# Block 1's transposes, the first W2 load and the order of VectorE's sums in the opening of a fused matmul-GELU-matmul kernel

## The chip, the cores and the metric

The kernel runs on one core of a Trainium2 chip. The metric is device time in microseconds (us) of one execution, the median of several. Each execution also reports its span, from first to last instruction, and the mean clock that was granted to TensorE, where 1.0 is full speed. The span is about 1.8 us shorter than the time. "PE" is TensorE, "PEld" its weight loads, "DVE" VectorE, "ACT" ScalarE, "POOL" GpSimd and "SP" the queue that issues most DMAs. bX, bY, bZ and bW are the banks of PSUM into which TensorE writes its products, and "arena" is the kernel's storage in SBUF.

## The reference

```python
def setup_inputs():
    batch, m, k, h, n = 16, 512, 768, 3072, 768
    # x (16, 512, 768), w1 (768, 3072), b1 (3072), w2 (3072, 768), all float32, random normal

def reference(x, w1, b1, w2):
    y = np.matmul(x, w1) + b1
    y = 0.5 * y * (1.0 + erf(y / np.sqrt(2.0)))
    return np.matmul(y, w2).astype(np.float32)
```

The 8192 rows of x are worked in eight blocks of 1024 rows. The change touches only the opening, in which blocks 0 and 1 are multiplied by W1.

## The kernel before

A block product is done with seven half-size products instead of eight (a Strassen-type scheme). This saves TensorE work and costs sums on VectorE. For x, they are S1, S2, a difference written over A21, and S4. For each W1 column tile there are four combinations, T1 to T4. A `Unit1` is one column tile of W1 times one block of x, and one call of `period` works on unit `i` and finishes unit `j`, the one before:

```python
            # period(i, j, fill), usual case
            p1(i); copy_xy(i)     # bX = A11*B11; ScalarE copies bX to bY
            p7(j)                 # bY of j += A21*T3; VectorE adds c22 (line 535)
            fill(1)
            p5(i)                 # bW = S1*T1; ScalarE copies bW out
            fill(2)
            p3(j)                 # bZ += S4*B22; VectorE adds c12 (line 562)
            fill(3)
            p6(i)                 # bY += S2*T2; VectorE copies bY to bZ (line 577), "the bZ copy"
            j.right_done(); fill(4)
            p4(j)                 # bY of j += A22*T4; GELU out of PSUM
            fill(5)
            p2(i); fill(6)        # bX += A12*B21; GELU out of PSUM
```

`p7` of the next period writes the bY bank that the bZ copy reads, so TensorE may not start it until that copy is done (TensorE waited 2.07 us for it in the longest case before). `fill(1)` to `fill(6)` put pending VectorE sums and DMA issues between the products. In the traces below VectorE works in the order in which the program gives it work, so a sum that waits for data holds back the bZ copy behind it (2.55 us in the largest case before the change).

```python
        def fill_a(pos, slot):                       # pos: place in the list of 24 Unit1 of blocks 0 and 1
            if slot == 1:
                if pos in (at[1, 0] - 2, at[1, 0] - 1):       # positions 5 and 6
                    h = pos - at[1, 0] + 2
                    x_sums(1, soon, slice(h * RH // 2, (h + 1) * RH // 2))   # sums of block 1
                if pos + 1 < len(seq) and seq[pos + 1][0] == 0:
                    prep_wt(seq[pos + 1][1])                  # T1..T4 of the next W1 tile
                ...
                for m, c in ((21, 9), (22, 0), (23, 3), (23, 6)):
                    if pos == m:
                        prep_w2(T2, c, queue)                 # combinations of W2
                ...
            elif slot in (1, 2, 4, 5):
                sums((0, 600, 300, 0, 600, 300)[slot])        # pop sums worth so many ns
            if slot == 5:
                loads_a(pos)
                if 1 <= pos < 5:
                    for t in (pos - 1, pos + 3):
                        transpose_dma(1, t)                   # one 128-row tile of block 1's x
            if slot == 6:
                flush(soon)
```

At this stage x, W1 and W2 come from HBM as float32 and are cast to float16 by DMAs that GpSimd issues. The row tiles of block 1 are then transposed from SBUF to SBUF by DMAs of SP, in the order 0, 4, 1, 5, 2, 6, 3, 7. The first half of block 1's sums needs the first four of them.

Of the kernel before, what the change touches and what calls it, by code (L numbers as in the profile page):

```python
# [10 lines left out]
P = 128  # L11
# [6 lines left out]
B11, B21, T1, B22, T3, T2, T4 = range(7)  # L18
# [4 lines left out]
def kernel(  # L23
# [8 lines left out]
    nc = tc.nc  # L32
# [5 lines left out]
    RH = SB // 2  # L38
    nsb = R // SB
    KQ = K // P // 2  # L40
    NH = H // P // 2
# [57 lines left out]
    def g_of(sb):  # L99
        return Gs[min(sb, 1)]  # L100
# [20 lines left out]
    def w1_op(wt, slot):  # L121
        raw = wt[:, 0:4 * KQ * P].rearrange("p (a k b c) -> p a b k c", a=2, k=KQ, b=2)
        if slot in RAW:
            return raw[:, RAW[slot][0], RAW[slot][1]]
        return wt[:, slot * KQ * P:(slot + 1) * KQ * P].rearrange("p (k c) -> p k c", c=P)
# [46 lines left out]
    bT = [pp.tile([P, 2 * KQ, P], F16, name=f"bT{k}") for k in range(2)]  # L172

    with tc.manual_schedule():

        soon, queue, late, slow = [], [], [], []

        def tt(o, a, b, op):
            nc.vector.tensor_tensor(out=o, in0=a, in1=b, op=op)  # L179

        def later(n, f, q=None):
            (queue if q is None else q).append((70 + n * 0.52, f))

        def sums(ns):

            for q in (soon, queue):
                while q and ns >= q[0][0] * 0.6:
                    ns -= q[0][0]
                    q.pop(0)[1]()

        def flush(q):
            while q:
                q.pop(0)[1]()
# [17 lines left out]
        def keep(n):  # L211
            nc.sync.dma_start(out=w1s[hi_of(n)][:], in_=wts[n])

        def prep_wt(n):
            o = {s: w1_op(wts[n], s) for s in range(7)}
            for d, a, b in ((T3, B22, T1), (T1, T1, B11), (T2, B22, T1), (T4, B21, T2)):
                later(KQ * P, lambda d=d, a=a, b=b: tt(o[d], o[a], o[b], SUB), soon)

        def load_w2(k, c0, c1):
            nc.gpsimd.dma_start(out=w2rows[k][:, c0:c1, :], in_=w2r[:, k, c0:c1, :])  # L220

        W2C = 3

        def prep_w2(d, c, q):
            a, b = {T1: (T3, B11), T2: (B22, T1), T3: (B22, T3), T4: (B21, T2)}[d]
            o = [w2v[s][:, :, c:c + W2C, :] for s in (d, a, b)]
            later(2 * W2C * N4, lambda: tt(*o, SUB), q)
# [49 lines left out]
        def xh_of(sb, t):  # L277
            if sb < ONE:
                return cut(sb * GR + GR // 2 + t * K, K)
            return xh_late[t % 3]  # L280
# [5 lines left out]
        def xT_of(sb, t):  # L286
            return XTs[sb][:, t // NU, :, (t % NU) * P:(t % NU + 1) * P]

        def transpose_dma(sb, t):
            nc.sync.dma_start_transpose(out=xT_of(sb, t), in_=xhs[t])  # L290

        def transpose_pe(t):
            for kc in range(2 * KQ):
                nc.tensor.transpose(out=bT[t % 2][:, kc, :], in_=xhs[t][:, kc * P:(kc + 1) * P],
                                    identity=ident[:])
            nc.scalar.copy(out=xT_of(0, t), in_=bT[t % 2][:])

        def blocks(sb):
            XT = XTs[sb]
            return [XT[:, a, c:c + KQ, :] for a in range(2) for c in (0, KQ)]  # L300

        def x_sums(sb, q, r=slice(0, RH)):
            A11, A12, A21, A22 = [a[:, :, r] for a in blocks(sb)]
            S1, S2, S4 = [a[:, :, r] for a in XSs[sb]]
            n = KQ * len(range(RH)[r])
            later(n, lambda: tt(S1, A21, A22, ADD), q)
            later(n, lambda: tt(S2, S1, A11, SUB), q)
            later(n, lambda: tt(A21, A11, A21, SUB), q)
            later(n, lambda: tt(S4, A12, S2, SUB), q)

        def g_sum(k, U, c0=0, c1=NH, q=None):
            G1, G2 = g_of(U // NU)
            r = slice(U % NU * P, (U % NU + 1) * P)
            g11, g21 = G1[:, c0:c1, 0, r], G1[:, c0:c1, 1, r]
            g12, g22 = G2[:, c0:c1, 0, r], G2[:, c0:c1, 1, r]
            s = [t[:, c0:c1, :] for t in GS]
            a, b, op = ((g21, g22, ADD), (s[0], g11, SUB), (g11, g21, SUB), (g12, s[1], SUB))[k]
            later((c1 - c0) * P, lambda: tt(s[k], a, b, op), q)
# [260 lines left out]
        def p2(u):  # L579
            u.mm(2, bX[u.g % 2], False, 0, u.C)  # L580
            u.alloc()
            u.left_done(0, bX[u.g % 2])
# [69 lines left out]
        def spin(n):  # L652

            for k in range(n):
                nc.tensor.matmul(out=warm[k % len(warm)][:], lhsT=zero[:, 0, 0:P], rhs=zero[:, 0, :],
                                 start=True, stop=True, skip_group_check=True)

        spin(9)
        for t in range(4):
            xhs[t] = xh_of(0, t)  # L660
            nc.vector.tensor_copy(out=xhs[t], in_=xf[:, t, :])
            transpose_pe(t)
            if t == 0:
                nc.tensor.transpose(out=bW[:, 0:2 * NH], in_=bf, identity=idf[0:2 * NH, 0:2 * NH])
                nc.scalar.copy(out=b1t[:], in_=bW[:, 0:2 * NH])
            spin(2 if t < 3 else 6)
# [8 lines left out]
        for t in range(4, 8):  # L675
            if t == 6:
                p2(first)
            transpose_pe(t)
            spin(2 if t < 7 else 6)
            x_sums(0, soon, slice((t - 4) * P, (t - 3) * P))  # L680
            flush(soon)


        seq = ([(0, k) for k in range(7)] +
               [(1, 0), (1, 1), (1, 2), (0, 7), (1, 3), (0, 8), (1, 4), (0, 9), (1, 6), (0, 10), (0, 11),
                (1, 5), (1, 10), (1, 11), (1, 7), (1, 8), (1, 9)])
        at = {u: n for n, u in enumerate(seq)}
        over = {7: 0, 8: 1, 9: 2, 10: 3, 11: 4}

        def load_next_x(sb, ts):  # L690
            for t in ts:
                load_x(sb, t)

        w2_at_pos = {7: (0, 0, 2), 9: (0, 2, 4), 11: (0, 4, 6), 13: (0, 6, 8),
                     at[1, 6] + 1: (0, 8, 10), at[1, 6] + 2: (0, 10, 12),
                     at[1, 5] + 1: (1, 7, 12), at[1, 10] + 1: (1, 0, 3), at[1, 11] + 1: (1, 3, 7)}

        def loads_a(pos):
            if pos == 0:
                load_wt(4)  # L700
                load_next_x(1, (0, 4, 1, 5))
                load_wt(5)
                load_next_x(1, (2, 6, 3, 7))
                load_wt(6)
            for n in range(7, NH):
                if pos == at[1, over[n]] + 1:
                    load_wt(n)
            if pos in w2_at_pos:
                load_w2(*w2_at_pos[pos])

        def fill_a(pos, slot):
            if slot == 1:
                if pos in (at[1, 0] - 2, at[1, 0] - 1):
                    h = pos - at[1, 0] + 2
                    x_sums(1, soon, slice(h * RH // 2, (h + 1) * RH // 2))
                if pos + 1 < len(seq) and seq[pos + 1][0] == 0:
                    prep_wt(seq[pos + 1][1])
                if pos == at[0, NH - 1] + 2:
                    for c in range(0, NH, W2C):
                        prep_w2(T1, c, queue)  # L720
                    for k in (0, 1):
                        g_sum(k, 0)
                for m, c in ((21, 9), (22, 0), (23, 3), (23, 6)):
                    if pos == m:
                        prep_w2(T2, c, queue)
                        prep_w2(T3, c, late if m == 23 else queue)
                if pos == 23:
                    for c in range(0, NH, W2C):
                        prep_w2(T4, c, late)
            if pos > at[0, NH - 1]:  # L730
                if slot in (1, 4):
                    sums((0, 1100, 0, 0, 1500)[slot])
            elif slot in (1, 2, 4, 5):
                sums((0, 600, 300, 0, 600, 300)[slot])
            if slot == 5:
                loads_a(pos)
                if 1 <= pos < 5:
                    for t in (pos - 1, pos + 3):
                        transpose_dma(1, t)
                if seq[pos][0] == 1:  # L740
                    keep(seq[pos][1])
            if slot == 6:
                flush(soon)
# [135 lines left out]
        for g, (kind, sb, k) in enumerate(units):  # L879
            cur = kind(g, sb, k) if g else first  # L880
            if g < len(seq):
                period(cur, prev, lambda slot: fill_a(g, slot))
            else:
                f = {Unit1: fill_mm1, Unit2: fill_mm2_one, Unit3: fill_mm2_two}[kind]
                period(cur, prev, lambda slot: f(sb, k, slot))
            prev = cur
# [30 lines left out]
```

## Time and profile before

The three runs at hand for the prediction had a median of 869.94 us (868.99 to 870.58). The profiled execution was 871.2 us with a span of 869.4.

These are lines of the profile page of before: the span, the engines' busy time, and the engines' shares of the chain that ended last ("issue" is time in which an engine waited for nothing that the profile shows; a "q" marks an engine's sequencer).

```profile
span 869.4 us, 16186 instructions
PE 853.5 (98%) x6298; PEld 560.2 (64%) x6298; DVE 653.0 (75%) x1114; ACT 418.9 (48%) x680; POOL 80.4 (9%) x131
...
PE 74%; DVE 14%; issue 6%; DMA 3%; ACT 1%; SPq 1%; POOL 0%; DVEq 0%; POOLq 0%
```

TensorE is the bottleneck, so only its gaps can be won. These lines are from the view of TensorE's waits: engine and line, what ended the wait, total us, number of times, and the longest.

```profile
PE bY L370 <- DVE bZ L577: 4.5, 4, 2.1
PE bY L462 <- DVE bZ L572: 2.1, 6, 0.3
PE bW L370 <- DVE arena L179: 1.5, 2, 0.8
```

The first line is the bZ copy, holding back `p7` four times. The longest of these waits is this one, in the timeline of TensorE (start, length, what, count, and in brackets the idle time before it):

```profile
40.50 1.46 PE L370 MATMUL bX<-arena 128*128 128x512 f16 x6
44.03 0.81 PE L370 MATMUL bY<-arena 128*128 128x512 f16 x3 [2.07 <-DVE bZ L577]
45.62 1.46 PE L370 MATMUL bW<-arena 128*128 128x512 f16 x3 [0.78 <-DVE arena L179]
46.87 1.49 PE L370 MATMUL bZ<-arena 128*128 128x512 f16 x3
48.15 1.74 PE L370 MATMUL bY<-arena 128*128 128x512 f16 x6
```

Two things are to be seen. TensorE idles 2.07 us and then 0.78 us. After that three matmuls take 1.46 us where they take 0.81 us elsewhere: the granted clock is halved for 3.4 us (0.50 from 45.3 to 48.7 us). The timeline of VectorE at the same place shows the cause of the first wait:

```profile
41.42 1.15 DVE L179 TENSOR_TENSOR arena<-arena 128x768 f16<-128x768 f16 x2 [2.55 <-DMA arena<-arena]
42.49 0.68 DVE L562 TENSOR_TENSOR arena<-bZ,arena 128x512 f32<-128x512 f32 x1
43.28 0.70 DVE L577 COPY bZ<-bY 128x512 f32<-128x512 f32 x1
43.88 2.07 DVE L179 TENSOR_TENSOR arena<-arena 128x768 f16<-128x768 f16 x5
```

VectorE stood 2.55 us in front of block 1's first sums, waiting for a transpose, with the bZ copy behind them. The same pattern, smaller, comes once with a W1 tile (63.17 us) and once with a W2 chunk (118.50 us). These are the lines of VectorE for the W1 tile and of TensorE for both:

```profile
63.17 1.14 DVE L179 TENSOR_TENSOR arena<-arena 128x384 f16<-128x384 f16 x3 [1.47 <-DMA arena<-in_w_dram]
...
65.77 0.81 PE L370 MATMUL bY<-arena 128*128 128x512 f16 x3 [0.98 <-DVE bZ L577]
...
121.39 0.81 PE L370 MATMUL bY<-arena 128*128 128x512 f16 x3 [0.99 <-DVE bZ L577]
```

The view by windows sums these places up (window; busy us of each engine, with counts; granted clock; DMA share; GB/s):

```profile
40.00:60.00 20.00, 17.15 (x73) 7.25 (x71) 12.78 (x23) 11.69 (x17) 0.85 (x1) 0.91 0.83 287
60.00:80.00 20.00, 19.02 (x89) 8.49 (x87) 10.71 (x20) 14.02 (x23) 4.61 (x6) 1.00 0.74 103
115.00:130.00 15.00, 14.01 (x65) 6.25 (x64) 10.75 (x17) 9.81 (x16) 0.78 (x1) 1.00 0.94 176
```

TensorE lacks 2.85, 0.98 and 0.99 us in them, and in the first one its clock averages 0.91.

### The profile page before, as it was taken

Reading aid. Unit: us, or ns where it says so; the run is one execution under the profiler, and the core shown is the slowest. Engines: PE = TensorE matmul, PEld = TensorE weight load, DVE = VectorE, ACT = ScalarE, POOL = GpSimd, SP = SyncE. Lnnn points to the kernel's source line nnn. Section 1 sums busy time; section 2 is a strip of 40 time slices with the busy share of each in tenths; the row PEclk is TensorE's granted clock in tenths of the full one; section 3 lists DMA queues with packets and bytes.
Section 4 is the critical chain, followed back from the end, with each engine's and each line's share of the span. In section 5 each row is a group of like instructions: output and inputs, shape, how many; then the busy total and the mean of one; then the engine's idle time right before and its main releaser. Section 6 shows DMA issues by size and latency. Waiting matters only on the chain.

```text
span 869.4 us, 16186 instructions
## 1 busy us (share of the span) xinstructions
PE 853.5 (98%) x6298; PEld 560.2 (64%) x6298; DVE 653.0 (75%) x1114; ACT 418.9 (48%) x680; POOL 80.4 (9%) x131
## 2 busy tenths in 40 slices
PE   8999999999999999999999999999999999999997
PEld 3434445666544699447984499644995459944797
DVE  5665577566446899579985799767996689957997
ACT  5667762111168612775127831477215771277511
POOL 5111010000100001100020000200002100010000
PEclk9999999999999999999999999999999999999999
DMA  9976794749979698995989979897898969967397
GB/s 226 187 251 104 216 186 156 260 171 268 224 219 293 187 325 322 287 308 178 319 300 268 285 242 329 277 313 189 292 334 267 331 152 321 355 216 259 109 300 270
DMA packets 144849, 219.42 MB, mean 252 GB/s; under 512 B 63276, under 2 KB 85732, under 8 KB 144772
## 3 DMA queue, kind: packets, MB, share of 16 engines
q1 hardware_dynamic: 119552, 181.01, 65.4%
q0 software_dynamic: 25184, 37.36, 20.4%
q8 instruction: 49, 0.80, 0.4%
q14 instruction: 28, 0.23, 0.1%
q10 hardware_dynamic: 36, 0.01, 0.0%
HBM read 180.30 MB, written 47.87 MB: 262 GB/s over the span
## 4 chain that ended last, share of the span: by engine, by line
PE 74%; DVE 14%; issue 6%; DMA 3%; ACT 1%; SPq 1%; POOL 0%; DVEq 0%; POOLq 0%
PE bY L370 17%; PE bX L370 11%; PE bY L462 10%; DVE arena L179 9%; PE bW L370 6%; PE bX L462 5%; PE bZ L370 5%; PE bY L410 5%; PE bX L410 4%; PE bZ L462 3%; PE bW L462 3%; PE bZ L410 2%; PE bW L410 2%; DMA arena<-in_w_dram 2%; DMA arena<-arena 1%
## 5 line engine op out<-in xcount | busy, mean ns | idle before, releaser
L179 DVE TENSOR_TENSOR arena<-arena 128x1536 f16<-128x1536 f16 (+6 forms) x628 | 393.8, 656 | 15.6 <-DMA arena<-arena 5.1
L370 PEld LDWEIGHTS <-arena 128*128 128x128 f16 x2016 | 196.9, 98 | 239.5 <-issue 10.1
L462 PEld LDWEIGHTS <-arena 128*128 128x128 f16 x3528 | 292.1, 98 | 12.6 <-issue 4.1
L370 PE MATMUL bY<-arena 128*128 128x512 f16 x864 | 219.2, 379 | 5.0 <-DVE bZ L577 4.5
L535 DVE TENSOR_TENSOR arena<-bY,arena 128x512 f32<-128x512 f32 (+1 forms) x104 | 70.8, 681 | 156.8 <-PE bY L370 107.5
L386 ACT ACTIVATE arena<-arena,b1t 128x1024 f16<-128x1024 f32 x96 | 110.3, 1149 | 66.4 <-DVE arena L562 66.4
L462 PE MATMUL bY<-arena 128*128 128x192 f16 x1512 | 139.7, 246 | 2.1 <-DVE bZ L572 2.1
L528 ACT COPY bY<-bX 128x512 f32<-128x512 f32 (+1 forms) x146 | 80.3, 550 | 127.4 <-DVE arena L504 90.4
L370 PE MATMUL bX<-arena 128*128 128x512 f16 x576 | 141.3, 379 | 0.0
L547 ACT COPY arena<-bW 128x512 f32<-128x512 f32 (+1 forms) x146 | 80.8, 553 | 94.9 <-PE bW L462 44.1
L410 PEld LDWEIGHTS <-arena 128*128 128x128 f16 x672 | 65.8, 98 | 44.2
L462 PE MATMUL bX<-arena 128*128 128x192 f16 x1008 | 92.0, 246 | 0.4
L562 DVE TENSOR_TENSOR arena<-bZ,arena 128x512 f32<-128x512 f32 (+1 forms) x104 | 70.4, 677 | 20.6 <-PE bZ L370 14.3
L370 PE MATMUL bW<-arena 128*128 128x512 f16 x288 | 78.5, 382 | 1.5 <-DVE arena L179 1.5
L370 PE MATMUL bZ<-arena 128*128 128x512 f16 x288 | 78.5, 382 | 0.0
L391 ACT ACTIVATE arena<-bX,b1t 128x512 f16<-128x512 f32 x96 | 65.3, 680 | 7.9 <-PE bX L370 7.9
L487 POOL DMA_DIRECT2D out_dram<-arena x42 | 30.5, 728 | 400.0 <-DVE arena L558 292.3
L391 ACT ACTIVATE arena<-bY,b1t 128x512 f16<-128x512 f32 x96 | 64.6, 673 | 0.0
L284 POOL DMA_DIRECT2D arena<-in_x_dram x60 | 32.4, 544 | 273.4 <-DMA arena<-arena 193.9
L577 DVE COPY bZ<-bY 128x512 f32<-128x512 f32 (+1 forms) x68 | 46.4, 682 | 6.3 <-PE bY L370 0.2
L410 PE MATMUL bY<-arena 128*128 128x384 f16 x288 | 49.6, 326 | 0.0
L462 PE MATMUL bW<-arena 128*128 128x192 f16 x504 | 49.0, 246 | 0.0
(41 smaller groups left out, 325.8 us busy)
## 6 DMA issues: line engine op xcount, KB each, us to landing
arena<-w2s SPq DMA_DIRECT2D x294, 288.0 KB, 4.6
arena<-w1s SPq DMA_DIRECT2D x72, 672.0 KB, 6.2
out_dram<-arena POOLq DMA_DIRECT2D x42, 384.0 KB, 5.0
w2s<-arena SPq DMA_DIRECT2D x49, 288.0 KB, 4.4
arena<-in_x_dram POOLq DMA_DIRECT2D x60, 192.0 KB, 6.8
w1s<-arena SPq DMA_DIRECT2D x12, 672.0 KB, 8.1
out_dram<-arena SPq DMA_DIRECT2D x21, 384.0 KB, 3.1
arena<-in_w_dram POOLq DMA_DIRECT2D x17, 384.0 KB, 6.0
```

The costliest lines, as they stand in the source:

```text
L179: nc.vector.tensor_tensor(out=o, in0=a, in1=b, op=op)
L284: nc.gpsimd.dma_start(out=xhs[t], in_=xr[:, sb * 8 + t, :])
L370: nc.tensor.matmul(out=dst[:, 0:RH], lhsT=w1_op(self.wt, slot)[:, c, :], rhs=a[:, c, :], start=first and c == 0, stop=c == self.C - 1, ski ...
L386: nc.scalar.activation(out=self.G[1][:, hi, :, :], in_=self.tmp, func=GELU, bias=b1t[:, 2 * hi + 1:2 * hi + 2])
L391: nc.scalar.activation(out=self.G[0][:, hi, row, :], in_=bank[:, 0:RH], func=GELU, bias=b1t[:, 2 * hi:2 * hi + 1])
L410: nc.tensor.matmul(out=dst[:, 0:N2], lhsT=a, rhs=w[:, :, c, :], start=first and c == 0, stop=c == self.C - 1, skip_group_check=True)
L462: nc.tensor.matmul(out=dst[:, t * N4:(t + 1) * N4], lhsT=a, rhs=w[:, c, :], start=first and c == 0 and t == 0, stop=c == NQ - 1, skip_grou ...
L528: nc.scalar.copy(out=bY[u.g % 2][:, 0:u.F], in_=bX[u.g % 2][:, 0:u.F])
L535: nc.vector.tensor_tensor(out=u.c22(), in0=bY[u.g % 2][:, 0:u.F], in1=w[:, 0:u.F], op=ADD)
L547: nc.scalar.copy(out=w[:, 0:u.F], in_=bW[:, 0:u.F])
L562: nc.vector.tensor_tensor(out=u.c12(), in0=bZ[:, 0:u.F], in1=w[:, 0:u.F], op=ADD)
L577: nc.vector.tensor_copy(out=bZ[:, 0:u.F], in_=bY[u.g % 2][:, 0:u.F])
```

## The change

The intent is to keep VectorE, and with it TensorE, from standing in front of late data in the opening. There are four parts:

- **PE**: row tiles 3 and 7 of block 1 are transposed by TensorE instead of DMA.
- **W2 late**: the first W2 load begins one position later, behind the load of the eighth W1 tile.
- **Order**: from position 7 on, the W1 combinations, and those of W2 except T1, move from slot 1 to slot 4 of their period, behind the c12 sum and the bZ copy. At position 5 the same rewriting puts the W1 combinations ahead of block 1's x sums.
- **Pairs**: block 0's x sums are made for two row tiles at a time, and the last two of them are put off.

```diff
-        def transpose_pe(t):
+        def transpose_pe(sb, t):
 ...
-            x_sums(0, soon, slice((t - 4) * P, (t - 3) * P))
-            flush(soon)
+            if t % 2:
+                x_sums(0, soon, slice((t - 5) * P, (t - 3) * P))
+                for k in range(4 if t < 7 else 2):
+                    soon.pop(0)[1]()
 ...
-        w2_at_pos = {7: (0, 0, 2), 9: (0, 2, 4), 11: (0, 4, 6), 13: (0, 6, 8),
+        w2_at_pos = {8: (0, 0, 2), 9: (0, 2, 4), 11: (0, 4, 6), 13: (0, 6, 8),
 ...
+        X1_PE = (3, 7)
+
         def fill_a(pos, slot):
-            if slot == 1:
-                ... x_sums, then prep_wt, then prep_w2 of T1, g_sum, prep_w2 of T2, T3, T4
+            if pos == at[1, 0] - 2 and slot in (2, 5):
+                transpose_pe(1, X1_PE[slot // 3])
+            if slot == (1 if pos < at[1, 0] else 4) and pos + 1 < len(seq) and seq[pos + 1][0] == 0:
+                s4 = [soon.pop(1)] if pos == 0 else []
+                prep_wt(seq[pos + 1][1])
+                soon[3:3] = s4
+            if slot == 4:
+                ... prep_w2 of T2, T3, T4
+            if slot == 1:
+                ... x_sums, prep_w2 of T1, g_sum
 ...
-            elif slot in (1, 2, 4, 5):
+            elif slot in (1, 2, 4, 5) and (pos, slot) != (0, 2):
 ...
-                        transpose_dma(1, t)
+                        if t not in X1_PE:
+                            transpose_dma(1, t)
```

More of the change, by code (lines that the diff above doesn't have):

```diff
@@ L295, in transpose_pe @@
                                     identity=ident[:])
-            nc.scalar.copy(out=xT_of(0, t), in_=bT[t % 2][:])
+            nc.scalar.copy(out=xT_of(sb, t), in_=bT[t % 2][:])
         def blocks(sb):
@@ L661 @@
             nc.vector.tensor_copy(out=xhs[t], in_=xf[:, t, :])
-            transpose_pe(t)
+            transpose_pe(0, t)
             if t == 0:
@@ L677 @@
                 p2(first)
-            transpose_pe(t)
+            transpose_pe(0, t)
             spin(2 if t < 7 else 6)
-            x_sums(0, soon, slice((t - 4) * P, (t - 3) * P))
-            flush(soon)
+            if t % 2:
+                x_sums(0, soon, slice((t - 5) * P, (t - 3) * P))
+                for k in range(4 if t < 7 else 2):
+                    soon.pop(0)[1]()
         seq = ([(0, k) for k in range(7)] +
@@ L709, in loads_a @@
                 load_w2(*w2_at_pos[pos])
+        X1_PE = (3, 7)
         def fill_a(pos, slot):
-            if slot == 1:
-                if pos in (at[1, 0] - 2, at[1, 0] - 1):
-                    h = pos - at[1, 0] + 2
-                    x_sums(1, soon, slice(h * RH // 2, (h + 1) * RH // 2))
-                if pos + 1 < len(seq) and seq[pos + 1][0] == 0:
-                    prep_wt(seq[pos + 1][1])
-                if pos == at[0, NH - 1] + 2:
-                    for c in range(0, NH, W2C):
-                        prep_w2(T1, c, queue)
-                    for k in (0, 1):
-                        g_sum(k, 0)
+            if pos == at[1, 0] - 2 and slot in (2, 5):
[5 more added lines that the diff above has]
+            if slot == 4:
                 for m, c in ((21, 9), (22, 0), (23, 3), (23, 6)):
@@ L729, in fill_a @@
                         prep_w2(T4, c, late)
+            if slot == 1:
+                if pos in (at[1, 0] - 2, at[1, 0] - 1):
+                    h = pos - at[1, 0] + 2
+                    x_sums(1, soon, slice(h * RH // 2, (h + 1) * RH // 2))
+                if pos == at[0, NH - 1] + 2:
+                    for c in range(0, NH, W2C):
+                        prep_w2(T1, c, queue)
+                    for k in (0, 1):
+                        g_sum(k, 0)
             if pos > at[0, NH - 1]:
```

## The prediction

> **What bounds the kernel.** TensorE. The page gives it 853.5 us busy of 869.4 (98%), and the chain that ended last is 74% PE. So only its gaps can be won. The timeline of PE shows 4.53 us between first-product starts (bX) of full-width units, except at five places, all before 130 us, each with DVE late:
> - Start: PE waits 0.72 us (at 16.53) for the x sums, and 0.49 us (at 19.13) for the bZ copy queued behind 23 small DVE operations.
> - 41.15 to 50.38: 9.23 us instead of 4.53, **4.70 too many**. DVE stands 2.55 us at 41.42 in front of block 1's first sums until the fourth of eight DMA transposes lands (41.3); the queued bZ copy holds PE 2.07 us, the W1 combinations 0.78 us. Then the granted clock is 0.5 for 3.4 us (nine matmuls at 0.43 us, not 0.22), about 1.7 us more. [...]
> - 63.97: period 5.75 us, **1.2 too many**: DVE meets the combinations of the eighth W1 tile (loaded 58.20 to 63.15) ahead of the c12 sum and the bZ copy.
> - 119.58: 5.77 us, **1.2 too many**: same pattern, W2 chunk landing at 118.5.
>
> **What changes.**
> 1. Two of eight transposes go to TensorE: 12 matmuls, 0.34 us for six in the start-up, so +0.68 us PE on the path, and two 0.80 us ScalarE copies.
> 2. The first W2 load (768 KB read, now issued at 25.74, in flight until about 39) comes after the eighth W1 tile. DMA is saturated to 38 us, so this and change 1 let transposes land sooner: four by about 39, six by about 41, instead of 41.3 and 43.6 for four and eight (estimate). The order listing also puts the first half of the sums after the bZ copy, about 41.
> 3. W1/W2 combinations pass behind the c12 sum and bZ copy from position 7 on. A free-running copy ends 0.25 us before the next period begins; first combinations (0.36 us each) are needed 1.3 us after, and a late load now meets 1 us of slack. The DVE work is unchanged.
> 4. Sums in pairs: 16 operations of 0.294 us (4.7) become 8 of about 0.55 (4.4). Two are deferred; the first bZ copy moves from 18.4 to about 17.6, and PE's second gap closes.
>
> **Sum.** -4.7 -1.2 -1.2 -0.8 (start) +0.68 (transposes) +0.25 (four sums in front of the c22 add and two in front of the next bZ copy at 41 to 46 just use up the slack; two copies on ScalarE in one period) = -7.0. The rest of the program is unchanged in order and bound by TensorE, so it shifts whole.
>
> **Predicted: 863.0 us, range 861.6 to 866.0; faster by over 2%: 0.01, within 2%: 0.97, slower by over 2%: 0.02.**
>
> **Right if:** PE's waits for the bZ copy fall from 4.5 to below 1 us; the clock stays 1.0 at 40 to 60 us; periods 5 and 6 take about 4.9 and 4.5 to 5.0; no 5.7 us period near 64 or 120; the first Unit 2 matmul (129.88) comes near 123; the tail from there has the same length.
>
> **Wrong if:** transposes still land late (after 42.5), so DVE stalls and the clock drops again: back to 867; the sums now packed around 41 to 46 hold the bZ copy or c22 add by more than 1 us; the sixth W1 tile (landing about 37.5), now first in DVE's order there, stops it; W2 loads, pushed back by 33 us, come late for their combinations near 115 to 128.

The 1.7 us inside the -4.7 is worked out from the trace (3.4 us at a clock of 0.5), and the sum comes to -7.0 us, or 863.0 from the median of 869.94. "Saturated to 38 us" rests on the view by windows of before, which gives a DMA share of 1.17 to 1.39 in every 2 us from 22 to 38 us.

## The result and the profile after

The changed kernel took 865.0 us (864.4 to 865.78, four runs), against 869.51 us for before in the same session. The ratio is 0.9947, with a 95% interval of 0.993 to 0.9964. Ratios here are the mean time of one kernel's fast runs over that of the other's in the same rounds, so they are not quite the ratio of the medians quoted. The time lies inside the predicted range. The gain is 4.5 us, where 7.0 were predicted.

These lines of the changed kernel's page answer to those of before:

```profile
span 864.0 us, 16201 instructions
PE 853.0 (99%) x6310; PEld 560.9 (65%) x6310; DVE 653.7 (76%) x1106; ACT 420.6 (49%) x682; POOL 80.4 (9%) x131
...
PE 82%; DVE 12%; issue 2%; DMA 2%; ACT 1%; SPq 0%; DVEq 0%; ACTq 0%
```

TensorE's waits:

```profile
PE bY L462 <- DVE bZ L572: 2.1, 6, 0.3
PE bY L655 <- DVE arena L641: 1.2, 1, 1.2
PE bT L294 <- DVE arena L661: 0.9, 1, 0.9
PE bX L370 <- DMA arena<-w1s: 0.6, 1, 0.6
PE bW L370 <- DVE arena L179: 0.4, 1, 0.4
```

The line of 4.5 us for the bZ copy is gone (the view leaves out idle times under 0.15 us). Timelines of TensorE, then of VectorE, at the place of the largest stall:

```profile
41.42 0.50 PE L294 MATMUL bT<-ident,arena 128*128 128x128 f16 x6
41.76 1.46 PE L370 MATMUL bX<-arena 128*128 128x512 f16 x6
43.05 0.81 PE L370 MATMUL bY<-arena 128*128 128x512 f16 x3
...
41.62 0.70 DVE L577 COPY bZ<-bY 128x512 f32<-128x512 f32 x1
42.23 2.35 DVE L179 TENSOR_TENSOR arena<-arena 128x384 f16<-128x384 f16 x5
```

The six transposing matmuls take 0.34 us of TensorE (41.42 to 41.76), and `p7` follows with no gap. The bZ copy now runs ahead of the sums. The same three windows are full, at full clock:

```profile
40.00:60.00 20.00, 20.00 (x98) 9.14 (x97) 14.00 (x26) 15.01 (x23) 2.29 (x3) 1.00 0.83 272
60.00:80.00 20.00, 20.00 (x95) 9.05 (x93) 12.76 (x25) 15.36 (x23) 3.87 (x6) 1.00 0.88 128
115.00:130.00 15.00, 15.00 (x78) 7.44 (x76) 10.96 (x16) 9.08 (x15) 0.71 (x1) 1.00 0.85 182
```

The three large stalls have vanished, and yet the median gained only two thirds of what was predicted. To find the rest, I cut each trace in three: from its start to the first product of x and W1 (first matmul of line 370 into bX), from there to the first matmul of block 0's second layer (line 410), and the rest. The change works mainly in the middle part.

| execution profiled | to the first product | first product to second layer | rest |
|---|---|---|---|
| before | 10.36 | 119.52 | 739.55 |
| before, run again | 10.99 | 117.69 | 739.74 |
| changed | 11.28 | 112.89 | 739.80 |
| changed, run again | 10.06 | 113.33 | 740.92 |

The middle part gained 6.63 us from the profile on which I had predicted (119.52 - 112.89). It gained only 4.80 us from a second profile of the very same kernel (117.69 - 112.89). So most of the difference is inside before itself, and not in a new cost of the change.

The last part is not quite untouched. It took 739.23 to 739.74 us in the seven profiles, here and below, of kernels with the early W2 load, and 739.57 to 741.53 us in the seven with the late one. In five of these seven TensorE waited once or twice, 0.27 to 1.7 us in all, for a load from w1s (W1's combinations, kept in HBM and loaded again) in the last part (0.57 us in the first profile of the changed kernel, 0.95 and 0.17 us in the second); in the seven profiles with the early load it never did. No run tests whether the late W2 load is the cause, and the medians don't show it: the change without the late load took 865.18 us, the change in the same session 865.36 us.

### The profile page after: what moved, and what is told of

It is laid out like the page before. It is cut to its first block, busy times and chain, and to the rows that moved or that the text cites. A ratio compares the mean times of both kernels' runs of the same rounds, so it can differ in the third digit from the quotient of the medians.

```text
span 864.0 us, 16201 instructions
## 1 busy us (share of the span) xinstructions
PE 853.0 (99%) x6310; PEld 560.9 (65%) x6310; DVE 653.7 (76%) x1106; ACT 420.6 (49%) x682; POOL 80.4 (9%) x131
## 4 chain that ended last, share of the span: by engine, by line
PE 82%; DVE 12%; issue 2%; DMA 2%; ACT 1%; SPq 0%; DVEq 0%; ACTq 0%
PE bY L370 21%; PE bX L370 14%; PE bY L462 10%; DVE arena L179 8%; PE bW L370 7%; PE bZ L370 6%; PE bX L462 6%; PE bY L410 5%; PE bX L410 4%; PE bZ L462 3%; PE bW L462 3%; PE bZ L410 2%; PE bW L410 2%; DMA arena<-w1s 1%; DVE bZ L572 1%
## 5 line engine op out<-in xcount | busy, mean ns | idle before, releaser
L179 DVE TENSOR_TENSOR arena<-arena 128x768 f16<-128x768 f16 (+4 forms) x620 | 393.8, 664 | 12.5 <-DMA arena<-arena 3.0
```

The costliest lines, as they stand in the source:

```text
L179: nc.vector.tensor_tensor(out=o, in0=a, in1=b, op=op)
```

## The experiments

Theory T1: the slow execution that I had profiled contained a drop of the clock that comes in only some executions of before, and I counted all of its cost as gain. Rival T2: the drop comes always, and the change gives 2 us back in new waits. A second question is which of the four parts does the work. Theory P says that the place in VectorE's order is what counts. Rival L says that it is the late landing of data, cured by fewer or earlier transfers.

All kernels gave correct results. Their times stand in a table at the end of this section. A "gap" below is the time between the starts of two successive matmuls beyond the usual one, so it is about 0.15 us longer than the idle time that the profile gives.

### Before, once more

No edit.

> The kernel before, unchanged, once more, to see how much of its own time moves from execution to execution. Theory T1 (my sum took the stalls of one profiled execution, 871.2 us, that was 1.3 us slower than the median, because the half-speed clock after the stall at 41 us comes only in some executions): the executions fall in groups 1 to 1.8 us apart, with mean clock near 0.997 in the slow group and 0.999 or more in the fast one. Rival T2 (the clock falls in every execution of before, and the change gives the missing 2 us back through new waits): every execution of before shows clock 0.997 and a time within 0.5 us of 870.

It took 870.3 us. Its profiled execution has the same stall of TensorE, but no slow matmuls after it:

```profile
44.48 0.81 PE L370 MATMUL bY<-arena 128*128 128x512 f16 x3 [1.88 <-DVE bZ L577]
46.07 0.82 PE L370 MATMUL bW<-arena 128*128 128x512 f16 x3 [0.78 <-DVE arena L179]
```

Of its six executions two had a mean clock of 0.997, the others 0.999 or 1.0. Over all three experiment sessions, before ran another 33 times beside the experiments: 12 executions (4, 3 and 5 of 11 by session, the third session on another chip) had a clock of 0.998 or less and a mean of 871.9 us, and 21 had 0.999 or more and a mean of 869.9 us. The groups are 2.0 us apart, a little more than expected. In 59 executions of the ten other kernels below, the changed one among them and the longer stall left out, the clock never fell below 0.999; in their profiles TensorE never stood longer than 1.66 us in the middle part. T1 holds and T2 falls. The groups overlap a little (the slow one begins at 870.8, the fast one ends at 871.35), because the start of the program varies too (10.36 and 10.99 us to the first product in the two profiles of before).

### A longer stall at the same place

```diff
-                if pos in (at[1, 0] - 2, at[1, 0] - 1):
-                    h = pos - at[1, 0] + 2
+                if pos in (at[1, 0] - 3, at[1, 0] - 1):
+                    h = 0 if pos < at[1, 0] - 1 else 1
```

> Before, with the first half of block 1's sums asked for one period sooner, so that VectorE, and with it TensorE, stands one period (4.5 us) longer in front of the same transposes. Theory T1 ([...] a longer stall always meets it): every execution shows clock 0.997 or less, and the time is 4.5 us plus about 1 us of clock above before's, 875 to 876.5 us. If the drop has nothing to do with the stall: still in about a third of the executions only, 874 to 875 us.

It took 875.36 us, with clocks of 0.996, 0.995, 0.996, 0.996, 0.995 and 0.998: a drop in every execution (the last is a smaller one than I had expected). In its profiled execution TensorE stood 6.14 us, and of the nine matmuls that followed, each three took 1.44 to 1.46 us instead of 0.81:

```profile
43.73 1.44 PE L370 MATMUL bY<-arena 128*128 128x512 f16 x3 [6.14 <-DVE bZ L577]
45.32 1.46 PE L370 MATMUL bW<-arena 128*128 128x512 f16 x3 [0.15 <-DVE arena L179]
46.58 1.46 PE L370 MATMUL bZ<-arena 128*128 128x512 f16 x3
```

Here is the view by windows from 40 to 60 us, in which the granted clock is the third number from the end. Before:

```profile
40.00:60.00 20.00, 17.15 (x73) 7.25 (x71) 12.78 (x23) 11.69 (x17) 0.85 (x1) 0.91 0.83 287
```

Before, run again:

```profile
40.00:60.00 20.00, 17.34 (x81) 7.63 (x79) 12.73 (x24) 12.69 (x20) 0.85 (x1) 1.00 0.95 290
```

The longer stall:

```profile
40.00:60.00 20.00, 16.12 (x66) 6.68 (x66) 13.94 (x27) 12.19 (x18) 0.00 (x0) 0.83 0.81 284
```

In the two profiles of before, idle times of 2.07 and 0.78 us came with the drop, and idle times of 1.88 and 0.78 us did not. With the longer stall, 6.14 us in its profile, the drop came in all six executions. So the drop goes with the stall, but what decides whether a stall of some 3 us brings it is not shown by these runs.

### One part alone

Order alone. TensorE transposes, W2 load and pairs are as in before:

```diff
+            if slot == (1 if pos < at[1, 0] else 4) and pos + 1 < len(seq) and seq[pos + 1][0] == 0:
+                prep_wt(seq[pos + 1][1])
+            if slot == 4:
+                ... prep_w2 of T2, T3, T4
             if slot == 1:
                 ... x_sums
-                if pos + 1 < len(seq) and seq[pos + 1][0] == 0:
-                    prep_wt(seq[pos + 1][1])
                 ... prep_w2 of T1, g_sum
-                ... prep_w2 of T2, T3, T4
```

> Before, with only the W1/W2 combinations later in their period (and, as a consequence of the same edit, block 1's x sums behind the W1 combinations at position 5); all eight transposes by DMA, W2 load early, start-up sums unpaired. Theory P (place in VectorE's order is what counts): the waits near 64 and 120 us vanish (2.4 us) and the one near 41 us shrinks from 2.2+0.9 us to below 0.6 us, because the sums now come behind the bZ copy at about 41 us, when the fourth transpose has just landed: 864 to 865.5 us. Rival L (late landing is what counts and only fewer or earlier transfers cure it): the stall at 41 us stays above 1.5 us, 867 to 868 us.

It took 865.74 us, a ratio of 0.994, which the noise does not tell apart from the whole gain of the change. Both waits near 64 and 120 us at the bZ copy were gone, and the clock did not drop in any of five executions. These are the waits of TensorE that remained or came:

```profile
PE bY L370 <- DVE bZ L577: 1.1, 2, 0.6
PE bX L370 <- DMA arena<-in_w_dram: 0.8, 1, 0.8
PE bW L370 <- DVE arena L179: 0.7, 1, 0.7
```

A wait of 0.6 us at the bZ copy came at 47.3 us, one period after the old stall, a little more than I had expected as a gap (0.72 against below 0.6). A new one came: the load of the eighth W1 tile took 6.6 us instead of 4.9, and the matmuls themselves stood 0.8 us in front of it. No other trace with the new order has that wait. The middle part took 114.16 us, about 1 us more than in the two profiles of the changed kernel; the two waits, 0.72 and 0.92 us as gaps, are enough for that. Theory P is right in what counts most; it came 0.2 us above its range, which is less than the spread of the executions.

TensorE transposes alone:

```diff
+            if pos == at[1, 0] - 2 and slot in (2, 5):
+                transpose_pe(1, X1_PE[slot // 3])          # X1_PE = (3, 7)
 ...
-                        transpose_dma(1, t)
+                        if t not in X1_PE:
+                            transpose_dma(1, t)
```

> Before, with only the two row tiles transposed on TensorE. Theory P: the four transposes that the first sums need still land after 40 us because the W2 load and the x loads are still in flight, and the sums still stand ahead of the bZ copy, so VectorE still stalls there by 1 to 2.5 us; 12 extra matmuls cost 0.68 us; 868.5 to 870.5 us. Rival L: the stall at 41 us is gone, 865.5 to 867 us.

It took 868.82 us, ratio 0.998. The fourth transpose landed at 41.0 us, VectorE stood 1.2 us, and gaps of 0.26 and 0.94 us stayed near 44, and 1.10 and 0.82 us at the two later places. Theory P.

The W2 load alone:

```diff
-        w2_at_pos = {7: (0, 0, 2), ...
+        w2_at_pos = {8: (0, 0, 2), ...
```

> Before, with only the first W2 load moved behind the eighth W1 tile. Theory P: transposes land 1 to 2.5 us sooner (39 to 40.3 instead of 41.3 for the fourth), VectorE's wait falls from 2.5 to 0.5 to 1.5 us, and the clock no longer falls: 866.5 to 868.5 us. Rival L: landing by 38.9, no stall left, 865 to 866 us. If the W2 load does not compete with the transposes: no change, 869 to 870 us.

It took 868.81 us, ratio 0.9979, just above theory P's range. The fourth transpose landed at 38.8 us instead of 41.3, as rival L had said. VectorE's wait for it fell from 2.55 to 0.43 us, and the gap at the bZ copy fell from 2.23 to 0.11 us. The gap of 0.95 us behind it stayed, because the sixth W1 tile's combinations still stood behind the sums, and so did the two later ones (1.40 and 1.28 us). The summary of the transposes' landing times in these two traces (min/median/max), before first, shows that the W2 load really was in their way:

```profile
DMA to landing us min/median/max: 2.8/6.1/14.1
```

```profile
DMA to landing us min/median/max: 2.8/4.4/11.0
```

A transpose of the same size takes 2.8 us from issue to landing when the cast loads are done, and the fourth one, issued among them, took 9.0 us. How the two kinds of transfer share the DMA engines, the traces don't show.

Only the place of block 1's first sums (two blocks of code exchanged at position 5):

```diff
-                if pos in (at[1, 0] - 2, at[1, 0] - 1): ... x_sums(1, ...)
                 if pos + 1 < len(seq) and seq[pos + 1][0] == 0:
                     prep_wt(seq[pos + 1][1])
+                if pos in (at[1, 0] - 2, at[1, 0] - 1): ... x_sums(1, ...)
```

> Before, with only two blocks of code exchanged, so that block 1's first x sums stand behind the W1 combinations, and with that behind the bZ copy, at position 5. Theory P: of the wait at 42 to 45 us (2.1+0.94) 0.5 to 0.9 us remains, as in the run with all of the order; the waits near 62 and 118 us stay at 1.0 to 1.4; no clock drop; 867.2 to 868.2 us. If the place of the sums is not what took that wait away in the run with all of the order: 869.5 to 870.5.

It took 868.72 us, ratio 0.9979, half a microsecond above theory P's range. Of the stall of 2.23 and 0.94 us, 0.95 us remained (at 47.5 us, in the next period), and the clock was 0.999 in all six executions, with no drop. The later gaps were 1.82 and 0.89 us, of which the first is larger than I had expected, because the eighth W1 tile came late again (its load took 5.6 us). So the exchange alone takes away two thirds of the largest stall, without a single transfer being earlier (the fourth transpose landed at 41.6 us), and no drop of the clock was seen.

### The change without one part

Without the new order, the other three parts kept:

```diff
-            if slot == (1 if pos < at[1, 0] else 4) and pos + 1 < len(seq) ...: s4, prep_wt
-            if slot == 4:
-                ... prep_w2 of T2, T3, T4
             if slot == 1:
-                ... x_sums, prep_w2 of T1, g_sum
+                ... x_sums, s4 and prep_wt, prep_w2 of T1, g_sum, prep_w2 of T2, T3, T4
```

> The changed kernel with VectorE's combinations back at their early place in the period (x sums ahead of the W1 combinations at position 5, W1 and W2 combinations ahead of the c12 sum), the TensorE transposes, the late W2 load and the pairs kept. Theory P (order is what counts): the transposes land by 39 us, so the wait for them is at most 0.4 us, but the wait of 0.95 us for the sixth W1 combination and the two of 1.0 to 1.4 us near 62 and 118 us stay: first product to Unit 2 about 116 us against 112.9, 867.8 to 868.8 us. Rival (the transposes and the load matter most): within 1 us of the changed kernel.

It took 867.44 us, ratio 0.9961. The transposes landed in time, and the middle part took 116.0 us as expected. The waits at the bZ copy came back at the two later places (as gaps 1.17 and 1.48 us):

```profile
PE bY L370 <- DVE bZ L577: 2.3, 2, 1.3
PE bW L370 <- DVE arena L179: 0.4, 1, 0.4
```

The wait for the sixth W1 tile's combinations was 0.27 us as a gap, not 0.95, which is enough to put the time 0.4 us below the range.

Without the TensorE transposes:

```diff
-        X1_PE = (3, 7)
+        X1_PE = ()
```

> The changed kernel with all eight transposes of block 1 by DMA again, the rest of the change kept. Theory P (VectorE's order and the W2 load's place are enough): with the W2 load late the eight transposes landed by 42.2 us in the run that had only that, and the sums now ask for the first four at about 42 and the rest at about 44.5, so nothing stalls, and the 12 matmuls saved give 0.5 to 0.9 us: 864.0 to 864.6 us against 865.0. Rival L (the TensorE transposes are what takes the stall away): a wait of 0.5 us or more comes back at 41 to 47 us and it is no faster than the changed kernel.

It took 865.27 us, ratio 0.9947: no better than the changed kernel, so the expected time was missed. The eight transposes did land by 42.6 us, and VectorE never stood in front of one. But with 0.68 us less matmul work in that period, the four sums in a row and the two after them now held the c22 add and the bZ copy, with gaps of 0.19 and 0.52 us. In this trace, what the transposes cost as matmuls is about what they gave VectorE as time: 0.68 against 0.71 us.

Without the late W2 load:

```diff
-        w2_at_pos = {8: (0, 0, 2), ...
+        w2_at_pos = {7: (0, 0, 2), ...
```

> The changed kernel with the first W2 load early again. Theory P: six transposes land by about 42.3 us as in the run with the TensorE transposes alone, sums ask at 42 and 44.5, so within 0.5 us of the changed kernel (864.6 to 865.6). Rival L: the stall of 0.5 us or more at 41 to 47 us returns, 865.8 to 867.

It took 865.18 us, ratio 0.9942, as theory P expected, with the same small gaps as the changed kernel and with transposes that landed at 42.4 us. With the new order in place, the later W2 load is not needed.

Without the pairs:

```diff
-            if t % 2:
-                x_sums(0, soon, slice((t - 5) * P, (t - 3) * P))
-                ...
+            x_sums(0, soon, slice((t - 4) * P, (t - 3) * P))
+            flush(soon)
```

> The changed kernel with block 0's sums by single row tiles as before. My prediction's step (0.8 us gained at the start): 865.8 us, the two start-up gaps of 0.9 and 0.66 us are back. What the first profile of the changed kernel shows instead (its start-up gaps are 0.59+0.31 us and a new one of 0.29+0.08 us follows near 23.7 us, so the pairs gain 0.3 us): 865.2 to 865.5 us, and no gap near 23.7.

It took 866.23 us, ratio 0.995 (0.9938 to 0.9962). The changed kernel in the same session had 0.9947 (0.9935 to 0.9959), so the times do not tell the two apart. The trace does not settle it by itself either: its start was disturbed by late loads of x, and 1.7 us of waits for two loads from w1s fell into its last part. What the other traces show is that with unpaired sums the two gaps at 15 to 18 us are 0.89 and 0.66 us (order alone, the W2 load alone, the exchange alone), and with pairs 0.59 and 0.31 us, followed by new ones of 0.28 and 0.08 us at 23 to 26 us (the changed kernel's first profile, and without the order, the TensorE transposes or the late W2 load). In the changed kernel's second profile late loads of x came first and the first gap is 0.35 us; the others are the same. That is 1.55 against 1.26 us, a gain of 0.3 us. In the run without pairs no gap is to be seen near 23.7 us, so the new gaps do belong to the pairs.

The changed kernel, once more (no edit):

> The changed kernel once more, to see its own spread. Theory T1 (start-up varies by about 1 us from execution to execution for reasons outside the change): executions between 864 and 866 us, mean clock 0.999 to 1.0, never 0.997; the first product of x and W1 starts anywhere from 9.7 to 11.3 us. Rival: it starts near 11.3 in every profile of the changed kernel, so the change delays the start.

It took 865.36 us, with clocks of 0.999 and 1.0. Its first product came at 10.06 us, after 11.28 in the first profile. The late start of the first profile is thus not an effect of the change. In nine executions of the changed kernel the clock never fell below 0.999.

### A version meant to beat both

All eight transposes go by DMA, the x sums of block 1 come two at a time, and the W1 combinations come behind the bZ copy from position 1 on:

```diff
-        X1_PE = (3, 7)
+        X1_PE = ()
 ...
-            if slot == (1 if pos < at[1, 0] else 4) and pos + 1 < len(seq) ...
+            if slot == (1 if pos in (0, 5, 6) else 4) and pos + 1 < len(seq) ...
 ...
-            if slot == 6:
+            if slot == 6 and pos not in (at[1, 0] - 2, at[1, 0] - 1):
                 flush(soon)
```

> A version meant to beat both: the changed kernel with all transposes by DMA (no extra matmuls), the first and second half of block 1's sums two at a time over four slots instead of four in a row, and the W1 combinations behind the bZ copy from position 1 on. Expected: the waits of 0.19 and 0.52 us at 44 to 46 us that the DMA-only version had and those of 0.29 and 0.08 us at 23 to 26 us vanish; first product to Unit 2 111.7 us against 112.9 of the changed kernel; 863.6 to 864.5 us. Rival: a new order makes a new wait of the same size, 865 us.

In the trace it did what it should: the gaps at 23 to 26 and at 44 to 47 us are gone, and the middle part took 111.95 us against 112.89. The time was 865.13 us, ratio 0.9934 (0.9919 to 0.9949), above the range that I had given, and the interval overlaps that of the changed kernel (0.9935 to 0.9959). It is a shorter program in one trace, but it was not shown to be a faster kernel. A difference of 0.9 us is less than what start-up alone varies by (the first product came at 11.28 and 10.06 us in the two profiles of the changed kernel).

| kernel | median us (lowest to highest) | ratio to before | 95% interval |
|---|---|---|---|
| before, again | 870.3 (868.77 to 871.68) | 0.9994 | 0.9979 to 1.001 |
| longer stall | 875.36 (874.98 to 877.09) | 1.0055 | 1.0039 to 1.0072 |
| order alone | 865.74 (864.56 to 866.08) | 0.994 | 0.9925 to 0.9955 |
| TensorE transposes alone | 868.82 (868.59 to 870.17) | 0.998 | 0.9965 to 0.9996 |
| W2 late alone | 868.81 (867.08 to 870.34) | 0.9979 | 0.9961 to 0.9996 |
| place of x sums alone | 868.72 (867.64 to 870.7) | 0.9979 | 0.996 to 0.9998 |
| change without order | 867.44 (866.76 to 868.23) | 0.9961 | 0.9945 to 0.9976 |
| change without TensorE transposes | 865.27 (864.43 to 867.28) | 0.9947 | 0.9935 to 0.996 |
| change without late W2 | 865.18 (864.42 to 865.73) | 0.9942 | 0.993 to 0.9954 |
| change without pairs | 866.23 (864.87 to 866.5) | 0.995 | 0.9938 to 0.9962 |
| change, again | 865.36 (864.92 to 866.11) | 0.9947 | 0.9935 to 0.9959 |
| spread version | 865.13 (864.54 to 865.81) | 0.9934 | 0.9919 to 0.9949 |

## Why the prediction was right or wrong

- **What bounds the kernel, and where the gaps are.** Right. TensorE was busy 98% and is now 99%, and the three places of 4.7, 1.2 and 1.2 us lost are gone from the trace.
- **"-4.7" at 41 us.** Right for the execution that I read, too large for the median. Of the 4.7 us, 2.23 + 0.94 were the two gaps and the other 1.5 the halved clock (3.4 us at half clock would be 1.7, but its first 0.3 us fell into a wait). That drop came in 14 of the 39 executions of before that the experiments counted (12 of 33 and 2 of 6). Without it the gaps measured 2.04 + 0.94, about 3.0 us. The step that failed is having subtracted stalls read from one execution of 871.2 us from a median of 869.94 us.
- **"-0.8 (start)".** The mechanism was right, but its size was not. The bZ copy did come earlier relative to the products, but the gaps of the start went from 1.54 us (0.88 + 0.66) to 1.27 us (0.59 + 0.31 + 0.29 + 0.08). One of the sums that were put off landed in front of the next c22 add and copy. This term measured 0.3 us.
- **The TensorE transposes, "+0.68".** Right: twice 0.34 us in the trace, and no other wait with them.
- **"+0.25" for the sums packed behind the bZ copy.** Nearly right: gaps of 0.10 and 0.08 us.
- **Transposes land sooner, "four by about 39, six by about 41".** Right: 39.1 and 40.5 us. But the stall at 41 us has two cures, of which this is one. The late W2 load alone took the gap at the bZ copy from 2.23 to 0.11 us (the 0.95 us behind it stayed), and all parts but the order left 0.27 us of the stall; with the transposes as late as before, the order alone left 0.72 us. At the two later places only the order helped. I had described the new order of the sums as a detail of the W2 load's part. In the experiments the time of the order alone can't be told from that of the whole change (0.994 against 0.9947). Without the order the other three together give 0.9961; the intervals overlap, but the middle part of the trace, 114.16 us with the order alone and 116.00 us without it, points the same way.
- **The combinations behind the bZ copy, "-1.2 -1.2".** Right. Those gaps at the bZ copy are in every kernel with the old order and in none with the new one.
- **The marks of being right.** The clock stayed at 1.0, and no period of 5.7 us is left. The second layer came at 124.17 us, not near 123, because that execution started 0.92 us later (11.28 against 10.36). I had put periods 5 and 6 at 4.9 and 4.5 to 5.0 us; they took 5.21 and 4.63 us, since both transposes stand in period 5. The tail from the second layer kept its length in the first profile (739.80 against 739.55 us), but took 740.92 us in the second.

The corrected sum for an execution of before without the drop, with the gaps of its second profile (2.04 + 0.94, 1.13 + 0.08 and 1.01 + 0.08 us at the three places), is -3.0 -1.2 -1.1 -0.3 +0.7 +0.2 = -4.7 us. It is an estimate from the numbers above, and the middle parts of the traces differ by as much (117.69 - 112.89 = 4.8). The medians gained 4.5 and 4.6 us in the two sessions in which the changed kernel ran (869.51 - 865.0, and 869.97 - 865.36). A median lies near the executions without the drop, as these are the majority (25 of 39), so the sum and the measured gain agree to about 0.2 us. The start varies from execution to execution by more than that (1.2 us between the two profiles of the changed kernel).

## What to carry to other kernels

When an engine that works in the order of the program serves the bottleneck, as VectorE does in these traces (its wait of 2.55 us for a transpose held back the bZ copy, and TensorE with it for 2.07 us), place work that waits for late data behind the work that the bottleneck needs next; here a change of order alone won, within the noise, as much as the order and three other measures together (0.994 against 0.9947). Before subtracting a stall from a median, check that the profiled execution is a typical one, and ask above all of a clock drop after a stall whether it comes in every execution (here in 14 of 39). Parts that each cure the same wait do not add up, so test each one alone and each one left out.
